# Projecting layer 0's first ten chunks from x before its norm, in a two-layer hybrid encoder

## The chip, the cores and the metric

The kernel runs on one core of one Trainium2 chip, in one launch. The metric is the device time of that core in microseconds (us). The kernel before took 885.38 us (median of three runs, 885.13 to 885.55).

The core's engines each have an instruction stream of their own, worked off in order: TensorE (PE, matmuls; PEld is its weight load), VectorE (DVE), ScalarE (ACT), GpSimd (POOL) and SyncE (SP, which here only issues DMAs). Where an instruction waits for another engine or a transfer, all that stands behind it on its engine waits as well.

## The reference, cut to what matters

The input is 256 tokens of width 1024; 16 learned meta tokens are put in front, so 272 tokens go through two layers and the 16 are dropped at the end.

```python
for layer in range(DEPTH):                                # 2 layers
    hn = rms_norm(h, norm_mix[layer])                     # h * rsqrt(mean(h*h) + eps) * gain
    proj = hn @ w_in[layer]                               # 1024 -> q 512, k 128, v 128, ssm 512, pool 512, gates 3*1024
    q = apply_rope(q); k = apply_rope(k)
    y_attn = windowed_gqa_attention(q, k, v, sink)        # 8 query heads, 2 kv heads, window 128
    y_ssm  = bidirectional_s5(u, lam, log_dt, b, c, d, glu_w, glu_b)
             # two scans over the tokens; z = gelu(y); z * sigmoid(z @ glu_w + glu_b)
    y_pool = multiscale_pool(p, pool_w, pool_scale)       # four window means, each times a 128x128 matrix
    branch = einsum(stack(y_attn, y_ssm, y_pool), w_branch)
    merged = sum(sigmoid(gates) * branch)                 # over the three branches
    h = h + merged @ w_out[layer]
    hn = rms_norm(h, norm_mlp[layer])
    h = h + relu(hn @ w_up[layer])**2 @ w_down[layer]     # 1024 -> 4096 -> 1024
return rms_norm(h, norm_final)[:, N_META:]
```

The norm's root is one number for each token, so it commutes with a projection: (x * rstd * gain) @ W = ((x * gain) @ W) * rstd. All of it is float32.

## The kernel before, in words

**Tiles.** Activations lie with channels on the 128 partitions and the 272 tokens on the free axis: x (`h`) is 8 tiles of 128x272, each projection result one tile. A float32 product is made of three matmuls in a faster format: every operand is split into a high part and the remainder, and `product` (L189) adds high weight x high x, high weight x low x, and low weight x high x in PSUM. So a chunk of 1024x128 weights times x is 8 x 3 = 24 matmuls of 272 columns.

**Weights.** All weights are chunks of 128x1024 floats (512 KB) in one list in the order of use. `need(i)` (L162) hands out chunk i, and before that issues the DMA of chunks up to three further (`AHEAD`, on SP) and the split of chunks up to two further (`SPLIT`): ScalarE copies the high part (L171), VectorE subtracts for the low part (L172). The raw, high and low buffers have three slots each.

**The order of work.** In layer 0 the chunks come as u0 to u3 (input of the state-space branch, SSM), k, v, q0 to q3, p0 to p3 (pooling), then the gates and branch matmuls of pooling, those of attention, the gates of the SSM, its GLU, its branch, w_out, and the MLP. Beside this main line run generators (`Side`, L234 to L264): `prep` makes the SSM's tables, quarter by quarter (transposes and small matmuls on TensorE, many small operations on VectorE), `scans` does the four scans, `attention` the attention. `pump` gives each of them a credit by its rate (`PREP0`, `SCAN0`, `ATT0`), and they emit their next piece while it lasts. Their matmuls keep their place in the program; a scheduler orders the other instructions by their readiness in its own model, except those that are pinned (`pin`).

**The prologue (L910 to L953).** SP loads x in four pairs of tiles while ScalarE's queue loads the SSM's `lam` and two tables. Five warm-up matmuls run on ones. Then the squares of x are summed by TensorE (`ss_m`), `stats` (L298) makes the root `rstd`, and for each tile xn = x * rstd (L937, VectorE), xh = xn * gain (L938, ScalarE) and xl = xn * gain - xh (L942, VectorE). VectorE works on the SSM's parameters (`ssm_params` L367, operations of 128x32) in its waits. Every projection of layer 0 takes xh and xl.

**The end of layer 0's scans (L740 to L771).** The fourth scan's matmuls make y in PSUM; ScalarE copies it (`yt`, L762), SP writes it to DRAM (`yd`) and reads it back in another layout (`yq`, L768), ScalarE applies gelu (`zt`, L769), and `split_z` (L1119) makes the high and low part `zs`, ScalarE and VectorE one each. The GLU's matmuls (`gl`) read `zs` of all four quarters; its result goes into the third branch (`br`), and that into w_out (`wo`).

Of the kernel before, what the change touches and what calls it, by code (L numbers as in the profile page):

```python
# [10 lines left out]
F32 = mybir.dt.float32  # L11
# [75 lines left out]
def encoder(ctx: ExitStack, tc: tile.TileContext, a: dict, out: bass.AP):  # L87
# [97 lines left out]
    def first_need(k):  # L185

        need(k - SPLIT, pinned=True)

# [168 lines left out]
    def params_load(l, eng):  # L357
# [7 lines left out]
        eng.dma_start(lams[l], a["lam"][l])  # L365
# [253 lines left out]
    SY.dma_start(dvec, a["d_vec"])  # L619
# [289 lines left out]

    with tc.high_priority():  # L910
        params_load(0, S)
        for k in range(4):
            SY.dma_start(h[:, 2 * k : 2 * k + 2, :], a["h0"][:, 2 * k : 2 * k + 2, :])
        S.dma_start(consts[:, C_ONE : C_ONE + P], a["consts"][:, C_ONE : C_ONE + P])
        S.dma_start(vecs, a["vecs"])

# [5 lines left out]
        parts = []  # L922
        sqs = slots(4, "sqs")
        for k in range(KT):
            if k == 1:
                V.tensor_tensor(sqs[:, k], h[:, k], h[:, k], ALU.mult)
            else:
                S.activation(sqs[:, k], h[:, k], AF.Square)
            parts.append(sqs[:, k])
        rstd, ia, iv = stats("m0", 0, parts)  # L930
    S.dma_start(consts[:, :C_ONE], a["consts"][:, :C_ONE])
    S.dma_start(consts[:, C_J:], a["consts"][:, C_J:])
    ctx.enter_context(tc.issue_after(ia))

    def first(k):
        xn = tmp(f"xn{k}")
        pin(V.tensor_tensor(xn, h[:, k], rstd, ALU.mult))  # L937
        S.activation(_r(xh[:, k]), xn, AF.Copy, scale=gain(0, k))  # L938
        return xn

    def second(k, xn):
        pin(V.scalar_tensor_tensor(_r(xl[:, k]), xn, gain(0, k), xh[:, k], ALU.mult, ALU.subtract))  # L942
# [12 lines left out]
    for l in range(DEPTH):  # L955
        t0 = 0 if l == 0 else NM
        N = NT - t0
        xs = [(xh[:, k, :], xl[:, k, :]) for k in range(KT)]
        xc = [(xh[:, k, t0:], xl[:, k, t0:]) for k in range(KT)]
# [12 lines left out]
        def proj(i, full=True, name=""):  # L972
# [17 lines left out]
        for i, q in enumerate(ORDER[l]):  # L990
            ps = proj(plans[l, "in"][i], name=f"u{q}")
            if l and i < 2:
                if i == 0:
                    rstd_l = stats(f"m{l}", 0, [ssq, sq7])[0]
# [446 lines left out]
```

## Time and profile before

| | |
|---|---|
| median of three runs | 885.38 us (885.13 to 885.55) |
| the profiled execution's own time | 886.54 us |
| its span in the profile | 884.7 us |
| TensorE matmuls | 858.8 us, 97% |
| TensorE weight loads | 788.0 us, 89% |
| VectorE | 662.9 us, 75% |
| ScalarE | 539.4 us, 61% |
| GpSimd | 4.1 us |
| DMA | 159.97 MB, mean 181 GB/s |

Busy time of matmuls overlaps: a row of a timeline that counts x24 gives their number, and the time from its start to its end is what they took together. In a timeline row the figures are start, duration, engine, line, operation, result <- operands, and, in brackets, the idle time before it and what released it. In the table of stretches each engine has its busy time and the number of its instructions, then follow the granted TensorE clock (1.00 is full, 2.4 GHz), the share of DMA and GB/s. The profile counts an fp32 matmul that isn't split as two passes, so the five warm-up matmuls show as x10.

### The profile page before, as it was taken

The page shows a single profiled execution, that of the slowest core. Times are in us where ns is not written, and L with a number is a line of the kernel's source. Part 1 is how long each engine was busy: PE and PEld are TensorE (multiplying, and loading weights), DVE is VectorE, ACT ScalarE, POOL GpSimd, SP SyncE. Part 2 cuts the span into 40 slices and gives each one's busy share as a digit, 9 for nine tenths or more (in the row PEclk, how much of TensorE's full clock was granted, in tenths as well). Part 3 has the DMA queues.
Part 4 walks back from the last instruction along what each step waited for, and adds up shares of the span by engine and source line. Part 5 has one row for each costly group of instructions (what it writes and reads, how often), then busy time and mean ns, then how long its engine had stood idle before and what let it go on. Part 6 is the DMA issues. An engine that isn't in the chain of part 4 may idle for free.

```text
span 884.7 us, 18107 instructions
## 1 busy us (share of the span) xinstructions
PE 858.8 (97%) x7050; PEld 788.0 (89%) x7050; DVE 662.9 (75%) x1440; ACT 539.4 (61%) x998; POOL 4.1 (0%) x32
## 2 busy tenths in 40 slices
PE   6999999999999999999999999999999999999996
PEld 5987777999799999999999878789999999999995
DVE  7988978999976558687887989687979644444555
ACT  5568597755467655487565466675565755555554
POOL 1000000000000000000000000000000000000000
PEclk8999999999999999999999999999999999999999
DMA  7644645554475556968656364625556555555551
GB/s 254 203 152 127 209 126 167 161 161 155 133 239 168 167 175 211 286 189 257 231 190 199 130 218 142 217 97 171 167 190 192 177 180 190 187 184 188 185 186 71
DMA packets 62086, 159.97 MB, mean 181 GB/s; under 512 B 20016, under 2 KB 24880, under 8 KB 62000
## 3 DMA queue, kind: packets, MB, share of 16 engines
q1 hardware_dynamic: 59552, 156.16, 54.8%
q10 hardware_dynamic: 2448, 2.65, 0.9%
q8 instruction: 55, 0.90, 0.4%
q14 instruction: 31, 0.25, 0.1%
HBM read 151.31 MB, written 7.47 MB: 179 GB/s over the span
## 4 chain that ended last, share of the span: by engine, by line
PE 69%; DVE 16%; ACT 6%; DMA 5%; issue 2%; SPq 1%; ACTq 0%; DVEq 0%
PE up L98 21%; PE dn L98 11%; PE acc L98 10%; PE pjg L98 7%; PE wo L98 5%; DVE lo L172 4%; PE br L98 4%; ACT hi L171 1%; PE pju L98 1%; PE y L98 1%; PE s L98 1%; DVE z L708 1%; PE pjp L98 1%; DMA yd<-yt 1%; DMA yq<-yd 1%
## 5 line engine op out<-in xcount | busy, mean ns | idle before, releaser
L172 DVE TENSOR_TENSOR lo<-raw,hi 128x1024 fp32r<-128x1024 f32 x240 | 292.9, 1222 | 156.9 <-ACT hi L171 156.2
L171 ACT ACTIVATE hi<-raw 128x1024 fp32r<-128x1024 f32 x240 | 253.6, 1058 | 227.1 <-PE up L98 76.1
L98 PE MATMUL up<-xh,hi 128*128 128x272 f32 (+1 forms) x512 | 146.6, 287 | 0.0
L98 PE MATMUL up<-xh,lo 128*128 128x272 f32 (+1 forms) x512 | 145.8, 285 | 0.0
L98 PE MATMUL up<-xl,hi 128*128 128x272 f32 (+1 forms) x512 | 145.5, 284 | 0.0
L98 PE MATMUL pjg<-xh,hi 128*128 128x272 f32 (+1 forms) x384 | 112.9, 294 | 0.9 <-DVE gates L1085 0.9
L98 PE MATMUL pjg<-xh,lo 128*128 128x272 f32 (+1 forms) x384 | 110.9, 289 | 0.0
L98 PE MATMUL pjg<-xl,hi 128*128 128x272 f32 (+1 forms) x384 | 110.8, 288 | 0.0
L98 PEld LDWEIGHTS up<-xl,hi 128*128 128x128 f32 x512 | 96.5, 189 | 1.5 <-DVE xl L289 0.4
L98 PEld LDWEIGHTS up<-xh,hi 128*128 128x128 f32 x512 | 96.3, 188 | 1.4
L98 PE MATMUL dn<-hid,hi 128*128 128x272 f32 x512 | 97.1, 289 | 0.0
L98 PEld LDWEIGHTS up<-xh,lo 128*128 128x128 f32 x512 | 96.4, 188 | 0.0
L98 PEld LDWEIGHTS dn<-hid,hi 128*128 128x128 f32 x512 | 80.5, 188 | 0.1
L98 PE MATMUL acc<-hi,ring 128*128 128x512 f32 x256 | 80.2, 395 | 0.0
L98 PEld LDWEIGHTS pjg<-xh,hi 128*128 128x128 f32 x384 | 72.5, 189 | 4.3 <-issue 3.2
L98 PEld LDWEIGHTS pjg<-xh,lo 128*128 128x128 f32 x384 | 72.4, 189 | 2.6 <-issue 2.2
L98 PEld LDWEIGHTS pjg<-xl,hi 128*128 128x128 f32 x384 | 72.4, 189 | 1.9 <-issue 1.5
L98 PE MATMUL dn<-hid,lo 128*128 128x272 f32 x256 | 74.1, 289 | 0.0
L98 PEld LDWEIGHTS acc<-hi,ring 128*128 128x128 f32 x256 | 46.0, 188 | 9.0 <-ACT ring L1271 0.4
L98 PE MATMUL acc<-lo,ring 128*128 128x512 f32 x128 | 50.3, 394 | 0.0
L98 PEld LDWEIGHTS dn<-hid,lo 128*128 128x128 f32 x256 | 48.2, 188 | 0.0
L98 PE MATMUL wo<-mgh,hi 128*128 128x272 f32 (+1 forms) x128 | 36.7, 288 | 1.3 <-ACT mgh L1166 0.7
(374 smaller groups left out, 1731.1 us busy)
## 6 DMA issues: line engine op xcount, KB each, us to landing
raw<-in_w_in_dram SPq DMA_DIRECT2D x76, 512.0 KB, 3.6
raw<-in_w_up_dram SPq DMA_DIRECT2D x64, 512.0 KB, 3.3
raw<-in_w_dn_dram SPq DMA_DIRECT2D x32, 512.0 KB, 3.5
raw<-in_w_dt_dram SPq DMA_DIRECT2D x32, 512.0 KB, 3.2
raw<-in_w_br_dram SPq DMA_DIRECT2D x24, 512.0 KB, 3.3
raw<-in_w_out_dram SPq DMA_DIRECT2D x16, 512.0 KB, 4.3
b<-in_b_row_dram SPq DMA_DIRECT2D x16, 256.0 KB, 5.2
b<-ffd SPq DMA_DIRECT2D x16, 256.0 KB, 5.0
```

Of the source, the lines that this page charges most:

```text
L98: i = nc.tensor.matmul(*args, **kw)
L171: S.activation(_r(hi), raws[j], AF.Copy)
L172: i_ = V.tensor_sub(_r(lo), raws[j], hi)
L708: V.tensor_tensor_scan(zv[:, t, 2 : n + 2], rho, xv[:, t].rearrange("p g j -> p (g j)"), 0.0, ALU.mult, ALU.add,)
```

## The change

Layer 0's first ten chunks (u0 to u3, k, v, q0 to q3) are projected from x times gain, without `rstd`: two new buffers `rawh` and `rawl` hold its high and low part, made by `take` as x comes in (`given` passes them to `proj`). x and the first three weights are loaded in turns, the first in halves, and split in `begin`. The squares are added on VectorE to two tiles, so that TensorE sums two instead of eight; this is done in place of u2's evacuation (`first_stats`), and by high priority. The first three results are kept unscaled and, once `rstd` is there, multiplied by it; so are the fourth, v, and the tables of cos and sin (by which q and k get theirs). q is projected on all 272 tokens. Beside each of q0 to q3, `normed` makes xn, xh and xl of two tiles; the pooling chunks p0 to p3 and all behind them read these, as before. The generators of the SSM's preparation and scans start behind u3 and not in front of u0. Some small loads change place: `lam`, `dvec` and the constants go to SP behind x and the first three weights. The halving of the GLU's bias is pinned.

```diff
-    def first_need(k):
-        need(k - SPLIT, pinned=True)
...
-        eng.dma_start(lams[l], a["lam"][l])
+        return eng.dma_start(lams[l], a["lam"][l])
...
-    SY.dma_start(dvec, a["d_vec"])
...
+    rawh, rawl = slots(0, "rawh"), slots(4, "rawl")
+    FIRST = 3
+    def begin(j, b0, b1):
+        if j not in made:
+            made[j] = tuple(wp.tile([P, 8, P], F32, tag=t, name=f"{t}{j}", bufs=3) for t in ("hi", "lo"))
+        hi, lo = made[j]
+        pin(S.activation(_r(hi[:, b0:b1]), raws[j][:, b0:b1], AF.Copy))
+        return pin(V.tensor_sub(_r(lo[:, b0:b1]), raws[j][:, b0:b1], hi[:, b0:b1]))
+    def take(k):
+        pin(S.activation(_r(rawh[:, k]), h[:, k], AF.Copy, scale=gain(0, k)))
+        return pin(V.scalar_tensor_tensor(
+            _r(rawl[:, k]), h[:, k], gain(0, k), rawh[:, k], ALU.mult, ALU.subtract
+        ))
+    def load(k):
+        pin(SY.dma_start(h[:, k : k + 2, :], a["h0"][:, k : k + 2, :]))
...
     with tc.high_priority():
-        params_load(0, S)
-        for k in range(4):
-            SY.dma_start(h[:, 2 * k : 2 * k + 2, :], a["h0"][:, 2 * k : 2 * k + 2, :])
...
+        pin(SY.dma_start(raws[0][:, :4], chunks[0][0][:, :4]))
+        load(0)
+        pin(SY.dma_start(raws[0][:, 4:], chunks[0][0][:, 4:]))
+        load(2)
+        for j in (1, 2):
+            pin(SY.dma_start(raws[j], chunks[j][0]))
+            load(2 + 2 * j)
+        pin(SY.dma_start(consts[:, C_ONE : C_ONE + P], a["consts"][:, C_ONE : C_ONE + P]))
+        pin(params_load(0, SY))
+        pin(SY.dma_start(dvec, a["d_vec"]))
+        pin(SY.dma_start(consts[:, :C_ONE], a["consts"][:, :C_ONE]))
+        pin(SY.dma_start(consts[:, C_J:], a["consts"][:, C_J:]))
...
-        parts = []
-        sqs = slots(4, "sqs")
-        for k in range(KT):
...
-        rstd, ia, iv = stats("m0", 0, parts)
...
+        begin(0, 0, 4)
+        take(0)
+        take(1)
+        begin(0, 4, 8)
+        take(2)
...
+        begin(1, 0, 8)
+        take(4)
+        take(5)
+        sq = slots(2, "sq")
+        for k in (0, 1):
+            pin(S.activation(sq[:, k], h[:, k], AF.Square))
+        for k in (6, 7):
+            pin(V.tensor_tensor(sq[:, k], h[:, k], h[:, k], ALU.mult))
+        def add(i, j):
+            return pin(V.tensor_tensor(sq[:, i], sq[:, i], sq[:, j], ALU.add))
...
+        begin(2, 0, 8)
+        take(6)
+        take(7)
+        pin(SY.dma_start(raws[3], chunks[3][0]))
+        for k in (2, 3, 4, 5):
+            pin(S.activation(sq[:, k], h[:, k], AF.Square))
+            add(0, k)
+        iv = begin(3, 0, 8)
+    def first_stats():
+        return stats("m0", 0, [sq[:, 0], sq[:, 6]])
-    def first(k):
+    def normed(k):
         xn = tmp(f"xn{k}")
-        pin(V.tensor_tensor(xn, h[:, k], rstd, ALU.mult))
+        V.tensor_tensor(xn, h[:, k], rstd, ALU.mult)
         S.activation(_r(xh[:, k]), xn, AF.Copy, scale=gain(0, k))
...
-    with tc.issue_after(iv):
-        for k in range(0, KT, 2):
-            xn = first(k), first(k + 1)
-            if k < 6:
-                first_need(k // 2)
-            second(k, xn[0])
-            second(k + 1, xn[1])
-    Side(prep(0), PREP0)
-    pump(BOOST)
-    first_pumps(iv)
+        V.scalar_tensor_tensor(_r(xl[:, k]), xn, gain(0, k), xh[:, k], ALU.mult, ALU.subtract)
...
+        given = [(rawh[:, k, :], rawl[:, k, :]) for k in range(KT)] if l == 0 else None
...
-            ws, x_ = need(i), xs if full else xc
+            ws, x_ = need(i), given or (xs if full else xc)
...
+        ahead = (FIRST, 2)[l]
         for i, q in enumerate(ORDER[l]):
-            ps = proj(plans[l, "in"][i], name=f"u{q}")
+            ps = proj(plans[l, "in"][i], name=f"u{q}", given=given)
+            if i < ahead:
+                if i == (ahead - 1, 0)[l]:
...
+                            rstd_l, ia, iv = first_stats()
...
-            if i == 0:
-                Side(scans(l), (SCAN0, SCAN1)[l])
+            if l and i == 0:
+                Side(scans(l), SCAN1)
...
+        if l == 0:
+            Side(prep(0), PREP0)
+            Side(scans(0), SCAN0)
+            pump(BOOST)
-        urgent(rope(proj(plans[l, "in"][4], name="k"), kr, 0, f"k{l}"))
+        urgent(rope(proj(plans[l, "in"][4], name="k", given=given), kr, 0, f"k{l}"))
...
+            if l == 0:
+                normed(2 * t)
+                normed(2 * t + 1)
...
-                S.activation(hb, glu_b(l, m), AF.Copy, scale=0.5)
+                pin(S.activation(hb, glu_b(l, m), AF.Copy, scale=0.5))
```

**What moves on VectorE.** Before, in VectorE's order, the eight xn and xl follow right on the root (L314 makes `rstd_m`, L937 xn, L942 xl), the SSM's parameters (`scratch`) stand ahead of it, and only the splits of weights (`lo`, L172) come between:

```order
L314 SCALAR_TENSOR_TENSOR rstd_m_116<-nt_m_118,rstd_m_116 128x272
L353 TENSOR_SCALAR scratch<-scratch 128x32
L437 TENSOR_TENSOR scratch<-scratch 128x32
L937 TENSOR_TENSOR xn_126<-h,rstd_m_116 128x272
L937 TENSOR_TENSOR xn_129<-h,rstd_m_116 128x272
L172 TENSOR_TENSOR lo_137<-raw_132,hi_136 128x1024
L942 SCALAR_TENSOR_TENSOR xl<-xn_126,vecs,xh 128x272
L942 SCALAR_TENSOR_TENSOR xl<-xn_129,vecs,xh 128x272
L937 TENSOR_TENSOR xn_142<-h,rstd_m_116 128x272
L937 TENSOR_TENSOR xn_145<-h,rstd_m_116 128x272
```

Now the same operations (xn at L983, xl at L985) stand among the parameters and rope (`qk`, L1059):

```order
L983 TENSOR_TENSOR xn_549<-h,rstd_m_248 128x272
L387 TENSOR_TENSOR scratch<-scratch 128x32
L388 TENSOR_TENSOR scratch<-scratch 128x32
L1059 TENSOR_TENSOR qk_304<-pjq_509,qk_304 128x272
L327 TENSOR_SCALAR scratch<-scratch 128x32
L398 TENSOR_SCALAR scratch<-scratch 128x32
L985 SCALAR_TENSOR_TENSOR xl<-xn_549,vecs,xh 128x272
L328 TENSOR_SCALAR scratch<-scratch 128x32
L399 TENSOR_SCALAR scratch<-scratch 128x32
L983 TENSOR_TENSOR xn_553<-h,rstd_m_248 128x272
L329 TENSOR_SCALAR scratch<-scratch 128x32
L403 SCALAR_TENSOR_TENSOR scratch<-scratch 128x32
```

From the root to the last xl the new order has 7 splits of weights, 8 xn, 8 xl, 20 further operations of 272 columns (u and v scaled, the tables, rope), and 114 operations of the parameters, 14 of them larger than 128x32.

**What moves on TensorE.** Before, the last scan's y of layer 0 (`y0_3`) stands between a gate's projection (`pjg`) and a branch of attention (`br01`), ahead of all of the GLU:

```order
L98 MATMUL pjg250_2806<-xh_70,hi43_2703 128x272
L98 MATMUL pjg250_2806<-xl_71,hi43_2703 128x272
L98 MATMUL pjg250_2806<-xh_70,lo43_2704 128x272
L98 MATMUL br016_2844<-ya0_443,hi44_2777 128x272
L98 MATMUL y0_3_2739<-st20_3_2656,b03_2012 64x68 x2
L98 MATMUL y0_3_2739<-ub_183,b03_2012 64x68 x2
L98 MATMUL y0_3_2739<-st20_3_2656,b03_2012 64x68 x4
```

Now it stands inside the GLU (`gl`), whose matmuls ahead of it read the quarters that are there:

```order
L98 MATMUL gl02_3011<-zs0_1838,hi48_2935 128x272 x2
L98 MATMUL gl02_3011<-zs0_1838,lo48_2936 128x272
L98 MATMUL y0_3_2899<-st20_3_2816,b03_2170 64x68 x2
L98 MATMUL y0_3_2899<-ub_315,b03_2170 64x68 x2
L98 MATMUL y0_3_2899<-st20_3_2816,b03_2170 64x68 x4
L98 MATMUL y0_3_2899<-ub_315,b03_2170 64x68 x2
L98 MATMUL y0_3_2899<-st20_3_2816,b03_2170 64x68 x4
L98 MATMUL gl00_2971<-zs0_1838,hi47_2870 128x272
L98 MATMUL gl01_2990<-zs0_1838,hi47_2870 128x272
```

Before, y0_3 has 969 matmuls of 272 columns of layer 0 ahead of it, now 1067; behind it 21 of the GLU's are left now. From the first w_out matmul on, the two orders are the same.

## Rows read from the trace of the kernel before

**Rows 1.** The page, part 1: busy us, share and instructions of each engine.
```profile
PE 858.8 (97%) x7050; PEld 788.0 (89%) x7050; DVE 662.9 (75%) x1440; ACT 539.4 (61%) x998; POOL 4.1 (0%) x32
```

**Rows 2.** Timeline, TensorE to 31 us: start, us, instruction, idle before.
```profile
1.14 4.90 PE L98 MATMUL warm_ps<-warm 128*128 128x272 f32 x10 [1.14 <-POOL warm L918]
5.83 4.28 PE L98 MATMUL ss_m<-sqs,consts 128*128 128x272 f32 x16
15.72 0.82 PE L98 MATMUL pju<-xh,hi 128*128 128x272 f32 x2 [5.61 <-ACT xh L938]
...
19.71 0.43 PE L98 MATMUL pju<-xh,hi 128*128 128x272 f32 x1
19.94 0.43 PE L98 MATMUL pju<-xl,hi 128*128 128x272 f32 x1
...
20.90 0.29 PE L98 MATMUL pju<-xh,lo 128*128 128x272 f32 x1
...
30.71 0.29 PE L98 MATMUL pjk<-xh,hi 128*128 128x272 f32 x1
```

**Rows 3.** Table of stretches; columns as in its heading line of the view.
```profile
core 0: us, PE busy (x) PEld busy (x) DVE busy (x) ACT busy (x) POOL busy (x), PEclk, DMA share, GB/s
...
5.00:10.00 5.00, 5.00 (x19) 3.75 (x17) 4.57 (x38) 1.96 (x6) 0.00 (x0) 1.00 1.01 339
15.00:20.00 5.00, 3.75 (x14) 3.27 (x15) 5.00 (x10) 3.84 (x11) 0.11 (x1) 0.50 0.36 125
...
55.80:208.40 152.60, 149.76 (x1434) 125.71 (x1434) 136.85 (x357) 108.19 (x223) 0.89 (x11) 1.00 0.51 155
```

**Rows 4.** Timeline, VectorE, prologue.
```profile
4.08 0.18 DVE L331 TENSOR_SCALAR scratch<-scratch 128x32 f32<-128x32 f32 x1 [3.19 <-DMA scratch<-in_lam_dram]
...
14.14 0.43 DVE L314 SCALAR_TENSOR_TENSOR rstd_m<-nt_m,rstd_m 128x272 f32<-128x272 f32 x1
...
14.68 0.78 DVE L937 TENSOR_TENSOR xn<-h,rstd_m 128x272 f32<-128x272 f32 x2
15.39 1.22 DVE L172 TENSOR_TENSOR lo<-raw,hi 128x1024 fp32r<-128x1024 f32 x1
16.52 0.91 DVE L942 SCALAR_TENSOR_TENSOR xl<-xn,vecs,xh 128x272 fp32r<-128x272 f32 x2
17.35 0.78 DVE L937 TENSOR_TENSOR xn<-h,rstd_m 128x272 f32<-128x272 f32 x2
```

**Rows 5.** Timeline, ScalarE: its first squares of x.
```profile
4.27 1.19 ACT L928 ACTIVATE sqs<-h 128x272 f32<-128x272 f32 x3 [0.63 <-DMA h<-in_h_dram]
```

**Rows 6.** Chain of waits, first 62 us and end of layer 0's scans: start, us, what.
```profile
9.37 0.10 DVE scratch L335
...
47.12 3.01 PE pjq L98 x24
...
52.38 3.41 PE pjp L98 x27
...
211.30 0.41 ACT yt L762
211.72 5.24 DMA yd<-yt
216.98 0.58 SPq L768
...
220.16 0.69 ACT zt L769
...
221.35 0.44 DVE zs L1121
```

**Rows 7.** Tiles yd, then yq, layer 0: issue to landing.
```profile
DMA to landing us min/median/max: 1.8/2.6/5.2
...
DMA to landing us min/median/max: 2.3/2.7/3.6
```

**Rows 8.** Timeline, TensorE: first GLU and first w_out matmul.
```profile
220.23 0.42 PE L98 MATMUL gl<-zs,hi 128*128 128x272 f32 x2
...
243.33 0.49 PE L98 MATMUL wo<-mgh,hi 128*128 128x272 f32 x1
```

More of the change, by code (lines that the diff above doesn't have):

```diff
@@ L907, in pooling @@
         yield 0.4, 0
+    rawh, rawl = slots(0, "rawh"), slots(4, "rawl")
[13 more added lines that the diff above has]
+        pin(SY.dma_start(h[:, k : k + 2, :], a["h0"][:, k : k + 2, :]))
     with tc.high_priority():
-        params_load(0, S)
-        for k in range(4):
-            SY.dma_start(h[:, 2 * k : 2 * k + 2, :], a["h0"][:, 2 * k : 2 * k + 2, :])
-        S.dma_start(consts[:, C_ONE : C_ONE + P], a["consts"][:, C_ONE : C_ONE + P])
+        for j in range(FIRST + 1):
+            raws.append(wp.tile([P, 8, P], F32, tag="raw", name=f"raw{j}", bufs=3))
         S.dma_start(vecs, a["vecs"])
+        pin(SY.dma_start(raws[0][:, :4], chunks[0][0][:, :4]))
[10 more added lines that the diff above has]
+        pin(SY.dma_start(consts[:, C_J:], a["consts"][:, C_J:]))
         warm = slots(1, "warm")
@@ L989, in encoder @@
         held = []
+        ahead = (FIRST, 2)[l]
         for i, q in enumerate(ORDER[l]):
-            ps = proj(plans[l, "in"][i], name=f"u{q}")
-            if l and i < 2:
-                if i == 0:
-                    rstd_l = stats(f"m{l}", 0, [ssq, sq7])[0]
-                keep = tmp(f"uk{l}{q}")
+            ps = proj(plans[l, "in"][i], name=f"u{q}", given=given)
+            if i < ahead:
+                if i == (ahead - 1, 0)[l]:
+                    if l:
+                        rstd_l = stats(f"m{l}", 0, [ssq, sq7])[0]
+                    else:
+                        with tc.high_priority():
+                            late.append(1)
+                            rstd_l, ia, iv = first_stats()
+                            late.pop()
+                        ctx.enter_context(tc.issue_after(iv))
+                keep = zt[:, i] if l == 0 else tmp(f"uk{l}{q}")
                 S.activation(keep, ps, AF.Copy)
                 held.append((q, keep))
-                if i == 1:
+                if i == ahead - 1:
                     rstd = rstd_l
@@ L1010, in encoder @@
         SY.dma_start(qk[:, 5:7], a["rope"])
-        if rstd is not None:
-            V.tensor_tensor(crs, crs, rstd, ALU.mult)
-            V.tensor_tensor(srs, srs, rstd, ALU.mult)
+        V.tensor_tensor(crs, crs, rstd, ALU.mult)
+        V.tensor_tensor(srs, srs, rstd, ALU.mult)
         def rope(ps, o, c0, name):
@@ L1051, in urgent @@
             return e
-        urgent(rope(proj(plans[l, "in"][4], name="k"), kr, 0, f"k{l}"))
+        if l == 0:
[3 more added lines that the diff above has]
+        urgent(rope(proj(plans[l, "in"][4], name="k", given=given), kr, 0, f"k{l}"))
         pump()
-        urgent(values(proj(plans[l, "in"][5], name="v")))
+        urgent(values(proj(plans[l, "in"][5], name="v", given=given)))
         pump()
         for t in range(4):
-            urgent(rope(proj(plans[l, "in"][6 + t], full=False, name=f"q{t}"), qr[t], t0, f"q{l}{t}"))
+            urgent(rope(proj(plans[l, "in"][6 + t], full=l == 0, name=f"q{t}", given=given), qr[t], t0, f"q{l}{t}"))
+            if l == 0:
+                normed(2 * t)
+                normed(2 * t + 1)
             pump()
+        if l == 0:
+            rstd = None
         side_att = Side(attention(l, kr, qr, vt, list(waits)), (ATT0, ATT1)[l])
```

17 lines of the change are left out of this document (4 added, 13 removed).

## The prediction, made before the run

> **What bounds the kernel now.** I read the page's busy shares first, then the table of stretches, then each engine's timeline of the first 40 us, then the chain of waits around the end of layer 0's scans. The page names TensorE: matmuls fill 97% of the span [rows 1]. What TensorE does not use is almost all in the prologue. After the five warm-up matmuls it sums the squares (ss_m from 5.83), stands idle for 5.61 us, begins the first projection at 15.72 with the clock at 0.50, and its matmuls start 0.23 us apart at 19.71, and later 24 take 3.01, 0.125 each; k, the fifth chunk, begins at 30.71 [rows 2, 3, 6]. VectorE is not idle meanwhile: from 4.08 it works on the SSM parameters, between and after the waits for x, and rstd follows at 14.14 [rows 4]. So the prologue's hole on TensorE is where VectorE does its parameters for nothing.
>
> Further on VectorE has little room. From 55.8 us (end of the first pooling projection [rows 6]) to 208.4 it is busy 136.9 of 152.6 us [rows 3]. At the far end of layer 0 the last scan's y leaves TensorE at 211.3, and its round trip (yt, DMA out, DMA in, gelu, the split zs) ends at 221.8 [rows 6, 7]. TensorE does not feel this: it works on projections until 220.2 and reaches the third quarter's share of the GLU as it arrives [rows 8].
>
> **The start.** The change issues 2.6 MB of weights and x in pieces, 256 to 512 KB each. The trace moved 339 GB/s from 5 to 10 us [rows 3], and the first pair of x tiles was in use at 4.27 [rows 5]; so x's last pair lands at about 10. My estimate for the first projection is 6.0, right behind the warm-up, and for the last raw low part 13.8 (two splits of 1.13, two pairs at 0.83 for rawl, and the sums of squares stand ahead of it in VectorE's order [rows 4]). Three chunks are 72 matmuls, 9.0 us at 0.125, spread over these arrivals: done at about 16. Four fp32 records of the sum of squares at 4.28/16 = 0.27 us [rows 2] add 1.1. ScalarE then copies two results, splits chunks 3 and 4 (1.06 each, taken as VectorE's 1.13) and takes the root: rstd at about 20.5, bounds 18 and 23. The fourth chunk ends about 20.4, where before it ended at 30.7: **10.3 us ahead**.
>
> **What VectorE owes next.** Behind rstd the new order puts, up to the last normalized low part xl: 7 splits of weights at 1.13 = 7.9; 20 operations of 272 columns at 0.355 (the four u and v scaled, cos and sin scaled, 13 of rope) = 7.1; eight xn at 0.355 = 2.8; eight xl at 0.415 = 3.3; 100 small parameter operations at 0.10 = 10; and 14 larger ones of up to 256 columns, between 0.10 and 0.355 each, taken at 0.2 = 2.8 [rows 4, 6]. The counts are of the new order; the prices are the distances between starts in VectorE's timeline (14.68, 15.39, 16.52, 17.35), and the row of the chain at 9.37 for a small one. Sum 33.9 us: xl is complete at 20.5 + 33.9 = 54.4. TensorE has six chunks of k, v and q in that time, 6 x 3.01, and some 2 us of swaps and transposes [rows 6]: ready at about 40.5. The next chunk, the first pooling projection, is the first that reads xh and xl. It must wait for them, some 14 us, and ends at about 54.8 where before it ended at 55.8. Of the 10.3 us 1.0 is left. Nothing covers this: TensorE takes its instructions in order, and all that stands behind is queued behind this chunk. With rstd at 18 the gain left is 3.5, at 23 it is -1.5.
>
> **What moves past the end of the scans.** Parameters now come after the u chunks, and with them the transposes (fft), all four preparations and all four scans stand later in TensorE's order: the last y stood behind 969 large matmuls of layer 0, now behind 1067. That is 98 more, 12.3 us at 0.125. Before, 155.5 us passed from the first pooling chunk's end to this y (55.8 to 211.3); now 167.8, so y ends at 54.8 + 167.8 = 222.6. Behind it stand only 21 matmuls of the GLU, all of which need z. The round trip, that lay beside projections, is now on the path: yt 0.41, issue 0.35, DMA out 2.6 (the median; this last one took 5.24 behind weights), issue 0.58, DMA in 2.7, gelu 0.69, zs on two engines 0.94 (220.85 to 221.79) = 8.2, bounds 7.2 and 11 by the shortest and longest landings [rows 6, 7]. z is ready at 230.8, against 221.8: 9.0 later.
>
> The Trainium skill (DMA: Bandwidth & Descriptors, Anatomy of one DMA) fits 2.0 us and the bytes over 436 GB/s per transfer, for transfers issued from GpSimd; 136 and 68 KB would then cost 2.3 and 2.2, and the forecast would fall by 0.8. These are issued from the sync queue, and the rows' medians stand.
>
> **After z.** From z to the first w_out matmul took 243.3 - 221.8 = 21.5 us [rows 6, 8]. Eighteen GLU matmuls are now done ahead, -2.3. But TensorE has stood still for 8 us, longer than the 5.61 that went before the 0.50 clock at 15 to 20 us [rows 2, 3], 1.2 of 2.4 GHz: I charge the 21 remaining at the lower level, 0.23 each as at 19.71, +2.2. The two nearly cancel, and the order from w_out on is the old one. The lower clock after the pooling wait is left out: most of that chunk's matmuls run while it waits anyway.
>
> **The edits that cost nothing by themselves.** q is projected in full, but in layer 0 both forms have 272 columns. Queue order: dvec, lam and the two tables leave ScalarE's queue for SP's, behind x; they are needed at the parameters, 20 us later. The rope table moves behind the cc and bc loads, weights 5 and 6, and is scaled after rstd; VectorE is late there anyway. Pinning glu_b's halving costs 0.2 us on an engine idle at that place. Bounds for each: 0 and 0.5 us.
>
> **Sum.** The profiled execution took 886.54 (span 884.7), 1.16 over the median of the runs, 885.38. 886.54 + 9.0 - 0.1 = 895.4, less 1.16 is 894.3. TensorE was idle 2.8 us from 55.8 to 208.4 [rows 3], some of it for the very scans that now come later; I take one off: **893**.
>
> **Rivals.** (a) *The head start is kept.* VectorE reaches the last xl before TensorE asks for it: then the first pooling projection ends at 40.5 + 3.4 = 44, 11.8 ahead, y at 211.8, z at 220.0, 1.8 earlier than before; with the 2.8 of short waits saved the kernel takes 885.4 - 1.8 - 2.8 = 881. For it speaks that TensorE is busiest of all and gets its work sooner. Against it: the count of operations behind rstd. It decides if they end before 44.
>
> By the Trainium skill (Perfetto Trace Analysis, Identifying the Most-Contended Engine) the engine with the highest occupancy is the one to improve, by which an earlier start of TensorE is worth what it saves, and this rival would be the forecast. The whole-span shares agree; the rows from 55.8 to 208.4, where VectorE is busy 90%, speak against it.
>
> (b) *The two cancel.* rstd comes at 18 (2.5 earlier), the round trip is at its shortest (1.0), the 2.8 of short waits are saved, and the clock stays up for the GLU (2.2): 894.3 - 8.5 = 886, no change.
>
> (c) *VectorE stays behind to the end.* In 55.8 to 208.4 it had 15.8 us idle [rows 3]. Parameters began at 4.08 before [rows 4] and the preparations follow from them; what of these now falls behind 54, and the waits for TensorE, can use up that room. If they do, the last scan's vector work ends some 4 us behind TensorE's order, y at 226, z at 235: 898.
>
> **How the numbers follow.** Forecast 0.55, (c) 0.13, (b) 0.14, (a) 0.18. A measurement here tells 0.2%, 1.8 us, from no change. Forecast and (c) are slower, 0.68; (b) the same, 0.14; (a) faster, 0.18. The forecast's own range is 889 to 898.5 (rstd 18 to 23, round trip 7.2 to 11). The range 880 to 900 takes in (b), (c) and the nearer half of (a), and leaves out what goes further.
>
> **What would show it.** Right: first projection near 6 us; k at 19 to 22; a long wait of the first pooling projection for xl or xh, ending near 54; y of quarter 3 at 217 to 225, and TensorE idle for 7 to 11 us behind it until zs; first w_out matmul at 247 to 254. Wrong: TensorE dense from 10 to 60 us, or first w_out matmul before 240.

## The result and the profile after

The changed kernel takes **906.16 us** (median of four runs, 903.58 to 908.27), the kernel before 885.25 beside it: a ratio of 1.0231, interval 1.0215 to 1.0247. It is slower, as forecast, but 13 us slower than the 893 forecast, and above the range's end of 900.

The profiled execution of after took 903.58 us, the fastest of the four. TensorE's timeline of it (columns as in [rows 2]):

```profile
5.45 0.81 PE L98 MATMUL pju<-rawh,hi 128*128 128x272 f32 x1
...
23.34 0.29 PE L98 MATMUL pjk<-rawh,hi 128*128 128x272 f32 x1
...
45.63 0.40 PE L98 MATMUL pjp<-xh,hi 128*128 128x272 f32 x1 [0.92 <-DVE qk L1059]
...
47.77 0.59 PE L98 MATMUL pjp<-xh,lo 128*128 128x272 f32 x1 [1.62 <-DVE lo L172]
...
52.90 0.39 PE L98 MATMUL pjp<-xl,hi 128*128 128x272 f32 x1 [1.04 <-DVE xl L985]
...
171.13 0.34 PE L98 MATMUL y<-st,b 128*64 128x68 f32 x4 [1.10 <-ACT st L744]
...
181.84 0.34 PE L98 MATMUL tp<-b,bz 128*48 128x80 f32 x2 [1.25 <-ACT bz L573]
...
191.76 0.39 PE L98 MATMUL pjg<-xh,hi 128*128 128x272 f32 x1 [0.80 <-ACT gates L1132]
...
228.34 0.34 PE L98 MATMUL y<-st,b 128*64 128x68 f32 x4 [1.53 <-ACT st L744]
...
231.75 0.41 PE L98 MATMUL y<-st,b 128*64 128x68 f32 x8
239.11 0.82 PE L98 MATMUL gl<-zs,hi 128*128 128x272 f32 x2 [6.95 <-ACT zs L1169]
241.22 0.59 PE L98 MATMUL gl<-zs,hi 128*128 128x272 f32 x1 [1.28 <-DVE zs L1170]
241.61 0.43 PE L98 MATMUL gl<-zs,lo 128*128 128x272 f32 x1
241.83 0.43 PE L98 MATMUL gl<-zs,hi 128*128 128x272 f32 x1
...
260.15 0.49 PE L98 MATMUL wo<-mgh,hi 128*128 128x272 f32 x1
```

The first projection starts at 5.45 instead of 15.72, and k at 23.34 instead of 30.71 [rows 2]. The pooling chunks (pjp), the first to read xl, then crawl: from 45.63 on they stop for rope, for low parts of weights, and for xl. At the far end TensorE stands still for 6.95 us for z, and the first w_out matmul is at 260.15 where before it was at 243.33 [rows 8]. That is 16.8 us; the two profiled executions differ by 17.0. So nearly all of the change's effect lies ahead of w_out.

VectorE's timeline of after (as [rows 4]):

```profile
4.45 0.69 DVE L915 TENSOR_TENSOR lo<-raw,hi 128x512 fp32r<-128x512 f32 x1 [4.45 <-ACT hi L914]
...
22.79 0.44 DVE L310 SCALAR_TENSOR_TENSOR rstd_m<-nt_m,rstd_m 128x272 f32<-128x272 f32 x1
...
27.20 0.20 DVE L327 TENSOR_SCALAR scratch<-scratch 128x32 f32<-128x32 f32 x1
...
57.62 0.91 DVE L985 SCALAR_TENSOR_TENSOR xl<-xn,vecs,xh 128x272 fp32r<-128x272 f32 x2
...
227.49 1.21 DVE L172 TENSOR_TENSOR lo<-raw,hi 128x1024 fp32r<-128x1024 f32 x1
228.63 0.71 DVE L742 TENSOR_TENSOR x<-x,tr 128x544 f32<-128x544 f32 x1
229.26 0.17 DVE L330 SCALAR_TENSOR_TENSOR scratch<-scratch 128x32 f32<-128x32 f32 x1
...
240.40 0.29 DVE L487 TENSOR_TENSOR gt<-scratch,scratch 64x128 f32<-64x128 f32 x1
240.72 0.44 DVE L1170 TENSOR_TENSOR zs<-zt,zs 128x272 fp32r<-128x272 f32 x1
```

The parameters (scratch) begin at 27.20, where before VectorE was at them from 4.08 [rows 4]; the last xl is complete at 58.5. At the end the last scan's x (L742, 228.63), which y waits for, stands behind a split of weights (lo, 227.49). From 229.26 on VectorE makes the parameters of layer 1, and the last zs stands behind them in its order.

The chain of y's round trip in after, ScalarE's rows and SP's (DMA issues):

```profile
232.20 0.40 ACT L757 ACTIVATE yt<-y 128x272 f32<-128x272 f32 x1 [1.50 <-PE y L98]
...
237.93 0.67 ACT L764 ACTIVATE zt<-yq 128x272 f32<-128x272 f32 x1 [0.32 <-DMA yq<-yd]
238.63 0.43 ACT L1169 ACTIVATE zs<-zt 128x272 fp32r<-128x272 f32 x1
```

```profile
232.62 0.33 SPq L759 DMA_DIRECT2D yd<-yt  x1
234.40 1.25 SPq L763 DMA_DIRECT2D yq<-yd  x2
```

The last y is ready at 232.2, its zs on ScalarE at 239.1 and on VectorE at 241.2.

Last, the table of stretches from the end of the pooling work to the last y, of before and of after (columns as in [rows 3]):

```profile
55.80:211.30 155.50, 152.64 (x1483) 128.23 (x1484) 139.72 (x361) 111.02 (x229) 0.89 (x11) 1.00 0.50 153
```

```profile
58.40:232.20 173.80, 165.46 (x1581) 140.99 (x1579) 155.05 (x385) 117.78 (x239) 0.89 (x11) 0.99 0.51 157
```

TensorE has 98 matmuls more in it (1581 against 1483), as the two orders said, and is idle for 8.3 us (173.80 - 165.46) instead of 2.9.

The same table from the start to the first w_out matmul, of before and of after:

```profile
0.00:243.33 243.33, 231.17 (x1972) 199.43 (x1972) 218.09 (x663) 155.03 (x323) 3.45 (x25) 0.99 0.54 168
```

```profile
0.00:260.15 260.15, 235.00 (x1959) 202.10 (x1960) 229.30 (x686) 157.88 (x328) 3.45 (x25) 0.96 0.51 159
```

TensorE is idle for 25.2 us of it instead of 12.2: 13.0 of the 16.8 us. The granted clock is 0.96 instead of 0.99, which is up to some 8 us more by these shares (0.04 of 260 less 0.01 of 243), an upper estimate, since part of it falls on idle time. On the other side the sum of squares has 12 records fewer, some 3 us at the 0.27 us each of [rows 2].

### The profile page after: what moved, and what is told of

It is laid out like the page before. It is cut to its first block, busy times and chain, and to the rows that moved or that the text cites. A ratio compares the mean times of both kernels' runs of the same rounds, so it can differ in the third digit from the quotient of the medians.

```text
span 901.8 us, 18125 instructions
## 1 busy us (share of the span) xinstructions
PE 862.4 (96%) x7038; PEld 790.9 (88%) x7038; DVE 674.5 (75%) x1464; ACT 542.3 (60%) x1004; POOL 4.1 (0%) x32
## 4 chain that ended last, share of the span: by engine, by line
PE 73%; DVE 14%; ACT 6%; DMA 4%; issue 2%; SPq 1%; ACTq 0%; DVEq 0%
PE up L98 21%; PE dn L98 11%; PE acc L98 10%; PE pjg L98 8%; PE br L98 6%; PE wo L98 5%; DVE lo L172 3%; PE pju L98 2%; PE pjp L98 2%; PE s L98 2%; PE yps L98 1%; DMA yd<-yt 1%; PE tp L98 1%; PE pt L103 1%; ACT hi L171 1%
## 5 line engine op out<-in xcount | busy, mean ns | idle before, releaser
L172 DVE TENSOR_TENSOR lo<-raw,hi 128x1024 fp32r<-128x1024 f32 x236 | 288.5, 1223 | 155.7 <-ACT hi L171 154.6
L171 ACT ACTIVATE hi<-raw 128x1024 fp32r<-128x1024 f32 x236 | 249.2, 1057 | 215.6 <-PE up L98 76.3
```

The lines of the kernel that those rows point to most:

```text
L171: S.activation(_r(hi), raws[j], AF.Copy)
L172: i_ = V.tensor_sub(_r(lo), raws[j], hi)
```

## The experiments

Two times of each profile are compared throughout: "p", where the first 24 pooling matmuls are through (the start of the 25th: 55.2 before, 58.0 after), and the end of the last y of layer 0 (211.3 and 232.2).

**e1, the order undone.** `lam` is loaded first on ScalarE's queue and the generators start in front of u0, as before.

```diff
-        pin(params_load(0, SY))
+        params_load(0, S)
...
+    Side(prep(0), PREP0)
+    pump(BOOST)
...
-            if l and i == 0:
-                Side(scans(l), SCAN1)
+            if i == 0:
+                Side(scans(l), (SCAN0, SCAN1)[l])
...
-            Side(prep(0), PREP0)
-            Side(scans(0), SCAN0)
```

> The changed kernel with one part undone: lam is loaded first again and the generators of the preparation and of the scans start in front of u0, as before; x is still projected without its norm. The last y of layer 0 then stands behind 975 large matmuls instead of 1071. Theory V (the postponed parameters and scans run VectorE and the scans late, and the last scan sets the end of layer 0): the last y leaves TensorE at 211 to 219 instead of 232, and the time falls to 884 to 893. Rival W (what counts is the stop in front of the first pooling projection, for xl): that stop stays about as long as it is, since the parameters still share VectorE with xn and xl, and the time stays at 900 to 906. Rival C (the lower clock after TensorE's stops): the time falls only by what the clock gives back, 3 to 5 us, to about 901.

893.40 us, ratio 1.0096 (1.0080 to 1.0111): 13 us of the 21 are gone, as theory V had it, time and last y just past its upper bounds of 893 and 219. The last y ends at 219.4, 13 earlier, w_out begins at 250.7. But the early start on x alone is still 8 us slower than before. p is at 54.0, hardly ahead of before's 55.2. (Here, and in e7 and e12 to e14, which build on e1, GpSimd sets the warm-up's ones later, the first projection starts at 6.4 to 7.1 instead of 5.45, and k at 23.9 to 24.1 instead of 23.3.)

**e2, normalization first.** `normed` for all eight tiles right behind the root, xn and xl pinned.

> The changed kernel, but the eight xn and xl are made right behind the root, pinned ahead of the parameters on VectorE. Theory V: the stop in front of the first pooling projection goes (that projection ends near 48 instead of 58), but VectorE owes the same work in all and the last y stands at the same place in TensorE's order, so it still ends at 226 to 232 and the time falls by no more than 5 us, to 900 to 906. Rival W: the ten us are kept to the end, 894 to 897.

903.14 us (1.0198, 1.0181 to 1.0214). The time went as V said; the last y came at 233.4, a little past V's 232. The step that V gave for it did not: p isn't at 48 but at 61.3. xl is complete at 45.6, but rope is now late on VectorE, and TensorE stops 5.96 us for k's swap (swk) instead. The wait moves along VectorE's order; whatever stands last there is waited for.

**e3, the postponement alone**, in the kernel before: the two `Side` lines and the first `pump` moved behind u3, nothing else.

> The kernel before with one part of the change alone: the generators of preparation and scans start behind u3. x is normalized first as before. The last y stands behind 1071 large matmuls instead of 973. Theory V: VectorE idles in the prologue and owes 13 us of parameters in the busy stretch, the last y ends at 222 to 230, its round trip is exposed, and the time is 895 to 905. Rival W: there is no stop in front of the first pooling projection here, so only the exposed round trip of some 7 us is paid at most, 885 to 892.

898.89 us (1.0151, 1.0136 to 1.0167), 14 us slower than before. p is at 59.0, the last y at 229.6, w_out at 257.5; time and last y are as V had them. TensorE stops in the last scans at the same places as in after, at some for as long and at some for less:

```profile
170.20 0.34 PE L98 MATMUL y<-st,b 128*64 128x68 f32 x4 [1.10 <-ACT st L749]
...
180.33 0.34 PE L98 MATMUL tp<-b,bz 128*48 128x80 f32 x2 [0.38 <-ACT bz L577]
...
190.28 0.39 PE L98 MATMUL pjg<-xh,hi 128*128 128x272 f32 x1 [0.81 <-ACT gates L1084]
...
225.81 0.34 PE L98 MATMUL y<-st,b 128*64 128x68 f32 x4 [0.42 <-ACT st L749]
```

So 1.10 and 0.8 in front of y and of the gate (171.13 and 191.76 in after) belong to the postponed order, not to VectorE's new work. In front of tp and of the last y it is 0.38 and 0.42 here, and 1.25 and 1.53 in after. From p to the last y TensorE is idle for 6.6 us in e3, 8.3 in after and 2.9 in before. e1 and e3 together (8 and 14) come close to the 21.

**e4, light parameters.** `exp_acc` of layer 0 returns a clamp, the steps of sine and cosine are cut.

> The changed kernel with less parameter work in layer 0: the polynomials of both exponentials, of sine and of cosine are left out (a clamp or one step stands for each), 50 to 60 VectorE operations of 128x32 fewer, 5 to 6 us at 0.10. Theory V (VectorE is the bound up to the last scan): the last scan comes 5 to 6 us earlier and the time falls by 4 to 7, to 899 to 902. Rival O (only the place in TensorE's order counts, 1071 matmuls, VectorE has room): the first pooling projection ends earlier, but the last y moves by less than 2 us, and the time by less than 2.

902.08 us (1.0202, 1.0181 to 1.0222). The time fell by 4, as V said; the last y came at 229.6, 2.5 us earlier, between V's 5 to 6 and O's 2. It settles nothing between them.

**e5, FLAG 6 instead of 16 in the changed kernel**, and **e6, PREP0 2.2 and SCAN0 3.0.** Both move the scans forward in TensorE's order, in two ways.

```diff
-FLAG = 16
+FLAG = 6
```

> The changed kernel with one number changed: the preparation's first transposes (fft) are emitted 6 pumps behind the parameters instead of 16 (FLAG). They then stand behind 254 large matmuls instead of 354, the last y behind 955 instead of 1071; VectorE has the same work. Theory M (the SSM's chain from fft to the last y runs at a fixed pace of about 158 us, as it did in before, after, e2, e3 and e4, so its start sets its end): fft comes at 58 to 65 instead of 75, the last y at 216 to 222 instead of 232, and the time falls to 889 to 897. Rival V2 (VectorE's total work sets the last y, as the 172 us of e1 suggest): the chain is stretched by what it starts earlier, the last y stays at 228 to 232 and the time at 900 to 906.

```diff
-PREP0 = 1.5
+PREP0 = 2.2
...
-SCAN0 = 2.0
+SCAN0 = 3.0
```

> The changed kernel with higher credits for the generators: PREP0 2.2 instead of 1.5, SCAN0 3.0 instead of 2.0. The chain starts at nearly the same place (fft behind 344 large matmuls instead of 354), but its last y stands behind 1003 instead of 1071. Theory M, if the pace is that of the credits: 68 matmuls fewer are 8.5 us, the last y at 222 to 226, the time 896 to 900. Rival V2 (the pace is VectorE's): the last y stays within 3 us of 232, TensorE waits more inside the scans, 902 to 906.

e5: 904.34 us (1.0220, 1.0191 to 1.0249), no gain, as V2 said, with the last y at 226.4, between the two theories. But now p is at 63.8. Where the side work was put among the projections, VectorE is busy nearly all the time, TensorE stands for 4.3 of 15.8 us, and the granted clock is 0.50 (stretch of e5):

```profile
48.00:63.80 15.80, 11.47 (x31) 7.36 (x32) 15.59 (x51) 8.09 (x21) 0.11 (x1) 0.50 0.27 88
```

So e5 moved the scans forward and lost the gain in front of p; as a test of M against V2 it is mixed. e6: 896.49 us (1.0132, 1.0101 to 1.0162), 10 us faster than the changed kernel, last y at 225.4, w_out at 252.6, as theory M had it. TensorE no longer waits for z: from 224 us to w_out its timeline has no stop over 0.2 us.

**e7 and e8, FLAG 6 in e1 and in the kernel before.**

> e1 (generators started in front of u0 again, x projected without its norm) with the 6 pumps of e5: fft behind 216 large matmuls, the last y behind 858. Theory M: the last y comes well ahead of the GLU, TensorE's main line keeps its start and is the bound, 876 to 884. Rival V2: VectorE is as busy as in e1, the last y stays near 215 to 218, and the time at 889 to 895.

> The kernel before with FLAG 6 instead of 16: fft behind 108 large matmuls instead of 228, the last y behind 857 instead of 973. A control: before, TensorE came to the GLU at 220.2 and the last z at 221.8, so by every theory an earlier chain can bring 2 us at most, and transposes or scans that stand too early for VectorE cost what TensorE waits for them: 883 to 890.

e7: 907.23 us (1.0242, 1.0224 to 1.0259), worse than e1 by 14; p is at 71.7. Both theories missed it. e8: 892.95 us (1.0084, 1.0069 to 1.0099), 7 slower than before and 3 beyond what was expected: the last y at 206.3, 5 earlier, but p at 60.9 and w_out at 250.4. Side work too early cost the main line here, as side work too late cost the scans in e3.

**e9 and e10, VectorE relieved by 24 us**, in the changed kernel and in before.

```diff
+                if 16 <= j < 58 and j % 2:
+                    made[j] = (hi, hi)
+                    continue
                 i_ = V.tensor_sub(_r(lo), raws[j], hi)
```

> The changed kernel without the low part of every second weight chunk among the gates and branches of layer 0: 21 chunks in which TensorE reads the high part twice, with as many matmuls. VectorE is relieved of 21 x 1.14 = 24 us, and the places in TensorE's order are nearly the same (last y behind 1060 large matmuls, 1071 in the changed kernel). Theory V2 (VectorE's work is the bound from 45 us to the last z): the last y comes at 215 to 222 instead of 232, the first w_out matmul at 244 to 251 instead of 260, the time is 888 to 896. Rival M (only the place of the scans and their pace in TensorE's order count): last y at 228 or later, 901 or more.

> The same relief (21 low parts, 24 us of VectorE) in the kernel before; last y behind 952 large matmuls instead of 973. Theory V2: TensorE and VectorE were in balance there, TensorE was idle some 5 us from 20 us to the first w_out matmul, so 2 to 5 us are to be had, 880 to 883; the changed kernel under the same relief (e9) stays 6 to 12 behind it, for the round trip of y that its order exposes. Rival M: no change, 884 to 886.

e9: 902.16 us (1.0166, 1.0137 to 1.0196), last y at 237.8; e10: 886.21 us (0.9996, 0.9983 to 1.0009), last y at 211.7. In e9's stretch VectorE is busy 140.20 us where it was busy 155.05 in after, and TensorE's idle time is no shorter (173.80 - 164.88 = 8.9):

```profile
58.40:232.20 173.80, 164.88 (x1512) 140.91 (x1511) 140.20 (x392) 115.14 (x235) 0.89 (x11) 0.95 0.51 154
```

That fells V2 as it was sized: it had 888 to 896 and a last y by 222. How much earlier the last y comes by the relief, this trace can't tell: it is of the slowest of e9's four executions (906.80, the others 900.74 to 903.51), and its clock in the stretch is 0.95 instead of 0.99, some 7 us of 173.80. By the times the relief is worth 4 us in the changed kernel (902.16 against 906.16; 6 by the two ratios) and nothing in before (0.9996). M, which looked beaten by e5, stands, as far as the place goes: from p to the last y it is 156.0 us in before, 157.1 in e10 and 156.2 in e13 (below), all with the order of before, and 174.1 in after, 170.7 in e3 and 178.2 in e9 (at the lower clock) with the postponed one. A fixed pace it is not in every kernel: e1 took 165.4.

**e11 and e12, low parts on GpSimd**, in the changed kernel, and in e1 together with a pin that holds layer 1's parameters behind w_out.

```diff
-                i_ = V.tensor_sub(_r(lo), raws[j], hi)
+                i_ = (PO if 16 <= j < 58 and j % 4 == 1 else V).tensor_tensor(_r(lo), raws[j], hi, ALU.subtract)
```

> The changed kernel, but 11 of the same chunks have their low part subtracted by GpSimd, which is idle, instead of VectorE (12.5 us fewer on VectorE; nothing is left out). No trace here shows what GpSimd takes for 128x1024. Theory V2: if it takes under 3 us each and VectorE isn't slowed meanwhile, the time falls by 5 to 10, to 896 to 901; if VectorE is slowed or TensorE waits for the low part, 904 to 912. Rival M: no gain in either case.

> e1 (generators started in front of u0 again) with the 11 low parts on GpSimd as in e11, and the parameters of layer 1 pinned behind w_out, where VectorE has room (they took 17 to 20 us of VectorE before the first w_out matmul in every run so far). Theory V2: VectorE is relieved of 12 us and more, TensorE's earlier start shows in the end, 879 to 887. Rival M: as e1, 890 to 895.

919.16 us (1.0360, 1.0328 to 1.0391) and 901.78 (1.0167, 1.0145 to 1.0189): worse by 13 than after, and by 8 than e1. That is beyond V2's 912 for e11 and M's 895 for e12. One cost shows where the two engines meet. GpSimd's, VectorE's and ScalarE's timelines of e11:

```profile
169.90 2.79 POOL L172 TENSOR_TENSOR lo<-raw,hi 128x1024 fp32r<-128x1024 f32 x1 [19.59 <-DVE z L703]
...
192.08 6.98 POOL L172 TENSOR_TENSOR lo<-raw,hi 128x1024 fp32r<-128x1024 f32 x1 [4.53 <-ACT hi L171]
```

```profile
170.53 2.19 DVE L709 COPY sm<-z 128x16 f32<-128x16 f32 x1
...
209.67 0.16 DVE L709 COPY sm<-z 128x16 f32<-128x16 f32 x1
```

```profile
168.76 1.06 ACT L171 ACTIVATE hi<-raw 128x1024 fp32r<-128x1024 f32 x1 [1.61 <-PE pjg L98]
```

A copy that takes VectorE 0.16 us took 2.19 and ended at 172.72, as GpSimd's subtraction did (172.69). That subtraction began 0.08 us behind ScalarE's high part (169.82), by the times the one that it reads; the scan (z) that its row names was not its input. The Trainium skill (SBUF — State Buffer, Who interferes with whom) says that the two engines share a pair of ports as an exclusive lock, which the first to issue holds for its whole instruction, and the row agrees. Ahead of the last y (248.2) four VectorE operations that met a subtraction took some 7 us longer than their like, an estimate from their rows. The rest of the loss is not shown: TensorE is idle for 15.0 us from p to the last y instead of 8.3, at a granted clock of 0.92 instead of 0.99, and this execution was the slowest of the four. What the pin of layer 1's parameters does by itself was not tried.

**e13 and e14: why is the early start worth nothing even in the old order?** e13 is e1 with the normalization first (as e2), by which fft and the four y stand in TensorE's order exactly where they stand in before; e14 is e1 with the relief of e9.

> e1 (order undone) with xn and xl made right behind the root, pinned. In TensorE's order fft and the four y stand exactly where they stand in the kernel before (228; 488, 621, 821, 973), so what is left of the change is the early start on x without its norm, and VectorE's new work. Theory M (the time from the first pooling chunk's end to the last y goes by the order, 155 to 157 us as in before and e10): if that chunk ends at 47 to 55, the last y comes at 203 to 211 and TensorE sets the end, 877 to 885. Theory D (VectorE's debt in the first 60 us: the parameters, xn, xl, rope and the new work are too much for it there, and the early start is lost in waits wherever they stand): waits before 60 us eat the ten us, the chunk ends near 55 or later and the time is 885 to 893.

> e1 with the relief of e9 (21 weight chunks of the gates and branches without low part, 24 us of VectorE, from the first gates on, behind 60 us). e1 took 162.8 us from the first pooling chunk's end to the last y, before 155.5, at nearly the same places. If VectorE's amount of work behind 60 us makes these 7 us, they go: last y at 209 to 212, 884 to 888. If the stops come from what VectorE owes before 60 us, or from steps that wait for each other, the time stays at 890 to 894.

e13: 896.68 us (1.0103, 1.0086 to 1.0120). From p (64.5) to the last y (220.7) it is 156.2 us, M's number; but p itself is 9 us later than before, as theory D said, and 4 us beyond D's range in time. Its stops, in TensorE's timeline:

```profile
36.16 0.36 PE L98 MATMUL pjq<-rawh,hi 128*128 128x272 f32 x1 [1.85 <-DVE scratch L437]
...
48.35 1.28 PE L98 MATMUL swk<-xek,consts 128*128 128x272 f32 x2 [8.94 <-ACT xek L1061]
...
51.31 0.60 PE L98 MATMUL pjq<-rawh,hi 128*128 128x272 f32 x1 [1.04 <-DVE qk L1062]
```

e14: 892.26 us (1.0062, 1.0039 to 1.0085), against e1's 893.40 (1.0096, 1.0080 to 1.0111): 1 us, or 3 by the ratios, whose intervals meet, where 5 to 9 were forecast. TensorE is idle for 11.1 us from p to the last y in e14 and 11.2 in e1. So the amount of work behind 60 us is at most a small part of it. In front of the pooling chunks VectorE has no room in after and e13. From the root to the last xl it is busy nearly without a break (stretch of after):

```profile
23.20:58.50 35.30, 29.29 (x189) 26.07 (x188) 34.96 (x159) 14.13 (x28) 0.11 (x1) 0.94 0.45 139
```

In e13 it is busy 26.70 of the 27.10 us from 23.80 to 50.90. And in the first 58 us as a whole it was busy 49.8 us before, 48.5 after, and 52.6 in e1 (table of stretches, before and then e1):

```profile
0.00:58.00 58.00, 50.38 (x316) 45.65 (x317) 49.84 (x176) 32.76 (x67) 2.44 (x13) 0.94 0.65 212
```

```profile
0.00:58.00 58.00, 49.61 (x305) 43.85 (x306) 52.63 (x193) 33.40 (x68) 2.56 (x14) 0.94 0.62 206
```

VectorE was already at work in the hole that TensorE had there. An earlier TensorE comes earlier to a wait for what VectorE makes. e13 pays all of it in front of p. e1 and e14, whose pooling chunks stand mixed in TensorE's order as in after, take 165.4 and 163.8 us from p to the last y; that this is the rest of the same debt is argued and not shown, and most of their stops there end with ScalarE (xh, p, yp, gates), whose own order no run changed.

**e15, the stop for z filled** with 14 matmuls that nobody reads.

```diff
+            dm = aux_tile("dummy")
+            for _ in range(14):
+                TE.matmul(dm[:, :NT], ident, h[:, 0], start=True, stop=True)
```

> The changed kernel with 14 fp32 matmuls of 272 columns added around the last y of layer 0, whose result nobody reads; they and the first 27 matmuls of the GLU, which now stand behind y, fill most of TensorE's 9 us of waiting for z. Rival C (the clock after the stop): the 21 matmuls behind z start 0.125 us apart instead of 0.23, 2.2 us less, and the time falls by 1 to 3, to 903 to 905, and varies less from run to run. Otherwise no change, or up to 2 us more where the added matmuls stand in the way of y.

904.31 us (1.0200, 1.0169 to 1.0231): inconclusive, the interval overlaps that of the changed kernel, and the runs spread as much (902.4 to 908.7). 2.2 us of stop were left, and the matmuls behind it were 0.23 apart all the same.

**e16 and e17, the hole of before's prologue filled** with ten and with seven matmuls on ones.

```diff
         rstd, ia, iv = stats("m0", 0, parts)
+        for _ in range(10):
+            pin(TE.matmul(ps[:, :NT], warm[:, 0, :P], warm[:, 0], start=True, stop=True))
```

> The kernel before with ten more warm-up matmuls on ones behind the sum of squares, so that TensorE doesn't stand still from 10.1 to 15.7 us. The places of fft and the scans are those of before. If the low clock at the first projection (0.50 from 15 to 20 us, matmuls 0.23 apart) comes from that stop and costs the path, the clock is up at 15.7, k begins 1.5 to 3 us earlier than 30.7, and the time is 882.5 to 884.5. If xl (complete at 24.6) or what VectorE owes in front of the first pooling chunk sets the pace there, k begins at most 1 us earlier and the time stays within 885 to 887.

> The same with seven instead of ten added matmuls: TensorE stands still for 1 to 2 us in front of the first projection. Same two cases as e16; if the clock is up with seven as well, its time is that of e16 or 0.5 less, since nothing can push the first projection back.

890.48 us (1.0051, 1.0036 to 1.0066) and 890.10 (1.0053, 1.0034 to 1.0071). e16's clock is up, and k begins at 30.58 instead of 30.71 (stretch and timeline of e16):

```profile
15.00:20.00 5.00, 2.90 (x17) 2.39 (x18) 5.00 (x10) 3.84 (x11) 0.11 (x1) 1.00 0.35 121
```

```profile
16.95 0.39 PE L98 MATMUL pju<-xl,hi 128*128 128x272 f32 x1 [0.95 <-DVE xl L945]
```

TensorE is faster there and waits for xl instead; VectorE is busy 5.00 of 5.00 us. The low clock of [rows 3] cost 0.13 us at k. Both are 4 to 5 us slower than before, a case that neither expectation had. By e16's trace 2.1 us of it are lost between p and w_out (245.4) and 3.0 behind w_out; why stays open. No version beat the kernel before.

## Why the prediction was right and wrong

The sign and the path were right, the sizes were not. By the steps of the prediction, forecast against the profile of after:

| step | forecast | measured |
|---|---|---|
| first projection; k | 6.0; 20.4 | 5.45; 23.3 |
| root; last xl | 20.5; 54.4 | 23.2; 58.5 |
| first pooling chunk's work done | 54.8 | 58.0 |
| from there to the last y | 167.8 | 174.1 (232.2) |
| round trip and zs | 8.2 | 9.0 (241.2) |
| z to w_out | 21.4 | 19.0 (260.2) |

**The start.** The root came at 23.2, at the upper bound of 23. TensorE's first three chunks were done at 19.4, not at 16 (from 11.35 to 13.4 its matmuls were 0.23 apart), and the sum of squares stands behind them in its order. With the root 2.7 us late, the chunk's end came 3.2 late. What VectorE owed next was sized right: 58.5 - 23.2 = 35.3 us against 33.9. That the pooling chunks wait for it was right too; but they stop bit by bit inside the first chunk, which starts at 45.63, and not once in front. (The 55.8 that the prediction took for this chunk's end before is the end of a row of 27 matmuls, which runs into the next chunk; the 24 were through at 55.2.)

**What moves past the end of the scans** is the step that failed, by its size. The 98 matmuls are there, and e3 and e1 show that the postponed order is worth 13 to 14 us, in either direction. The forecast carried 155.5 us over and added 12.3 for them, as if TensorE stayed as dense as it had been, and the sum then took one more microsecond off for short waits. In after TensorE is idle 8.3 us instead of 2.9 in this stretch: 5.4 us, and the sum of both terms, 12.3 + 5.4 = 17.7, is nearly all of the 18.1 by which the stretch grew (174.1 - 156.0). e3 has 3.7 of the 5.4 without the new work, so these come with the order; e9 has as much idle time with VectorE relieved, and e6, with 68 matmuls fewer in front of y, still 6.8 us. What in the order makes TensorE meet the last scans' steps before they are ready was not separated. The rows in front of the last y show one such place: in after its x stands behind a split of weights on VectorE (227.49 and 228.63). The lower clock behind the pooling stops, which the prediction left out, is there: from 58.0 to 59.8 us the matmuls of after are 0.23 apart, about 1 us in these rows alone.

**Rival (c)** came nearest in time (898) and was given 0.13. That is in part luck: its mechanism, VectorE's room used up, is a small part at most, since e9 gave VectorE 24 us back and won 4, and e14 won 1 to 3.

**The round trip** was right as a term: TensorE stood for z, 6.95 and 1.28 us. The transfers took 1.8 us (yd, 232.6 to the issue at 234.4), and 2.4 and 2.8 (the two of yq). By the fit of the Trainium skill (DMA: Bandwidth & Descriptors, Anatomy of one DMA), which is for transfers issued from GpSimd, the estimate was 2.3 and 2.2; the rows lie on both sides of it. What was missed is that zs on VectorE stood behind layer 1's parameters, ready on ScalarE at 239.1 and on VectorE at 241.2. **After z**, the 21 matmuls were at the lower level of 1.2 GHz, 0.23 us apart, as charged (the added matmuls of e15, meant to keep the clock up, left them at 0.23); the branch behind them took 14.5 us (245.7 to 260.2), where before it had stopped for ys as well and took 16.6 (226.7 to 243.3).

The miss of 13.2 us is then: 8.2 from the terms of the table (w_out at 260.2 instead of 252.2, and 0.2 behind it), 1.2 taken off for waits and by rounding, 1.2 because before's profiled execution lay over its median, and 2.6 because after's lay under its own.

**Rival (a)**, that TensorE's early start is kept, falls by e1 and e13: after is 10 us ahead at the first projection and 7.4 at k; at p it is 2.8 behind, e13 9.2 behind, and e1 1.2 ahead. The Trainium skill (Perfetto Trace Analysis, Identifying the Most-Contended Engine) would improve the engine with the highest occupancy first, and judges TensorE's headroom by its weight loads, among others. Here that was TensorE by both (matmuls 97%, weight loads 89%), and the runs disagree in so far as work handed to it earlier bought nothing: what it waits for next came from VectorE, busy 34.96 of 35.30 us between the root and the last xl.

## What to carry to other kernels

A hole on the busiest engine is worth filling only if the engines that feed it have room in the same stretch: list what they do during the hole before counting the hole as a gain. Where side work is threaded into a fixed order, its place in that order is a cost of its own: count the instructions that it moves behind, and then add the stops that the new neighbourhood brings, since an order that was dense before is not dense by itself. Relief of an engine tells more than its occupancy: VectorE was about 90% busy (155.05 of 173.80), and 24 us of its work taken out behind 60 us gave 4 us in the changed kernel, 1 to 3 in e14 and nothing in before. And a long stop can cost more than its length: behind the 6.95 us for z the matmuls were 0.23 us apart instead of 0.125.

## What the runs showed of the hardware that was not expected

GpSimd took 2.35 to 6.98 us for a subtraction of 128x1024 that VectorE does in 1.22, and a VectorE copy that met one took 2.19 us instead of 0.16, both ending within 0.03 us of each other. TensorE's matmuls were 0.23 apart in after at 11 to 13 us, behind stops of no more than 0.57 us, and the granted clock of 10 to 15 us was 0.66. The runs of the changed kernel spread by 4.7 us (903.6 to 908.3), those of e5 and e15 by 6, those of the kernel before by 0.5 to 4.8 in the series beside them. The longest runs of the changed kernel, e5 and e15 have the lowest mean granted clock and the shortest the highest (after: 0.986 in 903.58 us, 0.980 in 908.27); where in the kernel the clock was lost in the longer runs is open, since the trace of after is of the shortest.
